# Seven block products instead of eight for half of the K chunks of gate, up and down in a decoder block

## The chip, the core and the metric

One core of a Trainium2 chip runs the whole kernel. The metric is the device time of one execution in microseconds. TensorE multiplies, VectorE (DVE) and ScalarE (ACT) do elementwise work, GpSimd (POOL) can do elementwise work on SBUF, and SyncE (SP) issues the loads.

## The reference

A decoder block for 256 tokens: two attention branches, gates, a merge, then a dense FFN and a last norm. The change concerns the FFN:

```python
hn = rmsnorm(h, ffn_norm[l])                                    # h (256, 2048)
h = h + (jax.nn.silu(hn @ w_gate[l]) * (hn @ w_up[l])) @ w_down[l]   # w_gate, w_up (2048, 5632), w_down (5632, 2048)
return rmsnorm(h, final_norm)
```

## The kernel before

All values are float32. Each product is made of three float32r passes: an operand is cut into hi (its float32r rounding) and lo = operand - hi, and hi*hi + lo*hi + hi*lo are summed in PSUM. The activations are the stationary operand, transposed, in tiles of 128 K rows by 128 tokens; there are two token tiles. The weights stream past them in slabs of 512 columns.

A *job* is one slab: its K rows (16 tiles of 128 in gate and up, 44 in down) for both token tiles, summed in two PSUM banks `acc`. A *step* is two K tiles of a job: 2 K tiles x 2 token tiles x 3 passes = 12 matmuls (L805 for hi of the weights, eight of them; L810 for lo, four). A *group* is four K tiles (two steps) loaded by one DMA of 1 MB into one of four `raw` buffers (`load`, L722). `split` (L731) makes the weights of one step ready: ScalarE casts `raw` to `wh` (L742) and VectorE subtracts to get `wl` (L743). There are four buffers each of `wh` and `wl`, and the split of step s + 3 is issued at step s, so it can start when step s - 1 is done with its buffer. The last split of a group frees `raw`, and the next load into it is issued.

The order on each engine is the order in which the Python loop at L789 issues: at each step first the split of step s + 3, then what `later(d, fn)` has put down for this step, then the matmuls. Each engine works through its own instructions in that order; an instruction that waits holds up all behind it on the same engine.

What comes after a slab: `wout_done` (L582) adds the output projection to h in `xt`, takes the sums of squares, and two and three steps later transposes h on TensorE (`transpose4`, tile `hT_tp`), from which ScalarE and VectorE make `hh` and `hl`. `gate_ff_done` puts silu of the gate slab into `sil`; `up_done` multiplies with the up slab, and two and three steps later `sil` is transposed (`aT_tp`) and cut into `ah`, `al`, which stay in SBUF for down. `down_done` adds to `xt`. The last six steps run for one token tile, then for the other (`TAIL`).

Of the kernel before, what the change touches and what calls it, by code (L numbers as in the profile page):

```python
# [62 lines left out]
def block_kernel(ctx: ExitStack, tc, x, positions, attn_norm, w_in, q_norm, w_uq, kv_norm, w_ukv,  # L63
# [8 lines left out]
    work = ctx.enter_context(tc.tile_pool(name="work", bufs=2))  # L72
# [14 lines left out]
    # ------------------------------------------------------------------ setup  # L87
# [25 lines left out]
    # mask: [tri | 0 | tri], added to scores [q, k]  # L113
    mask = const([P, 3, P], "mask")
# [17 lines left out]
    # ------------------------------------------------------------ small helpers  # L132
    def rstd(ss, n, name):
        """ss [P, NT, m] partial sums of squares over n elements -> [P, NT] of 1/rms, in two parts."""
# [20 lines left out]
    def split_out(src, hi, lo, scale=None):  # L155
        """src -> hi + lo (float32r), scale a [P, 1] factor per partition."""
# [7 lines left out]
    def transpose4(nat, hi, lo, name, key=None, k0=0, nk=4, j0=0, first=False):  # L164
        """columns j0*128 .. nk*128 of nat [P tok, NT, :] -> hi, lo [P, :, S] at the same j, times the gains."""
# [22 lines left out]

    def rope(o1, o2, x1, x2, c, s, shape, name):
# [72 lines left out]
    # ------------------------------------------------------------ streams  # L262
    jobs = []

    def job(w, kt, lhs, done, name):
        jobs.append(dict(w=w, kt=kt, n=w.shape[1], lhs=lhs, done=done, name=name))

# [10 lines left out]
    # ------------------------------------------------------------ phase 1: x -> xT, projections  # L278
# [22 lines left out]

    L = {}
# [63 lines left out]
    # ------------------------------------------------------------ attention  # L366
    yT = {}
    PT = [const([P, 2, 512], f"PT{i}", F32R) for i in range(2)]
# [66 lines left out]
    # MLA head pairs  # L435
# [76 lines left out]
    # MoBA: SEQ == MOBA_BLOCK, so every query's own block is block 0 and no past block exists  # L512
# [45 lines left out]
    # ------------------------------------------------------------ branches, merge, FFN  # L558
# [7 lines left out]
    mh, ml, hh, hl = [], [], [], []  # L566
    ssh = const([P, NT, 4], "ssh")
    ssf = const([P, NT, 4], "ssf")
    R["h"], h_root, h_invert = rstd(ssh, D, "rstd_h")

# [11 lines left out]
    def wout_done(c):  # L582
        def done(ps):
# [4 lines left out]
            hh.append(big([P, 4, S], f"hh{c}", F32R))  # L588
            hl.append(big([P, 4, S], f"hl{c}", F32R))
# [6 lines left out]
    ah, al_ = [], []  # L596

    def gate_ff_done(c):
        def done(ps):
            s = L["sil", c] = big([P, NT, 512], f"sil{c}")  # L600
            for t in range(NT):
                nc.scalar.activation(s[:, t], ps[t], AF.Silu, scale=R["h"][:, t:t + 1])
        return done

    def up_done(c):
        def done(ps):
            s = L["sil", c]
            for t in range(NT):
                nc.vector.scalar_tensor_tensor(s[:, t], ps[t], R["h"][:, t:t + 1], s[:, t], op0=OP.mult, op1=OP.mult)
            ah.append(big([P, 4, S], f"ah{c}", F32R))  # L610
            al_.append(big([P, 4, S], f"al{c}", F32R))
            spread(2, s, ah[c], al_[c], f"aT{c}")
        return done
# [10 lines left out]
    def down_done(c):  # L624
        def done(ps):
            h = xt[c]
            for t in range(NT):
                nc.vector.tensor_add(h[:, t], ps[t], h[:, t])
                sumsq(h[:, t], ssf[:, t, c:c + 1])
                nc.vector.tensor_mul(h[:, t], h[:, t], L["gf"][c // 2][:, c % 2])  # L630
        return done

    def begin_norm():
        nc.vector.tensor_reduce(out=vf, in_=ssf[:, :, 0:3], axis=mybir.AxisListType.X, op=OP.add)
        nc.vector.tensor_scalar(vf, vf, EPS * D, None, op0=OP.add)
        nc.scalar.activation(warm, warm, AF.Sqrt)

# [23 lines left out]
    # ------------------------------------------------------------ the list of products  # L661
# [32 lines left out]
    for c in range(11):  # L694
        job(w_gate[:, 512 * c:512 * (c + 1)], 16, lhs_of(hh, hl), gate_ff_done(c), f"ga{c}")
        job(w_up[:, 512 * c:512 * (c + 1)], 16, lhs_of(hh, hl), up_done(c), f"up{c}")
    for c in range(4):
        job(w_down[:, 512 * c:512 * (c + 1)], 44, lhs_of(ah, al_), down_done(c), f"dn{c}")

    # ------------------------------------------------------------ issue  # L700
    groups, steps = [], []
    for jb in jobs:
        jb["step0"] = len(steps)
        k0 = 0
        while k0 < jb["kt"]:
            nk = min(2 if len(groups) < 2 else 4, jb["kt"] - k0)
            gi = len(groups)
            groups.append((jb, k0, nk))
            for k in range(k0, k0 + nk, 2):
                steps.append(dict(job=jb, k0=k, g=gi, off=k - k0, end=k + 2 >= k0 + nk, toks=(0, 1), src=len(steps)))  # L710
# [3 lines left out]
    steps[-TAIL:] = [dict(st, toks=(t,)) for t in range(NT) for st in tail]  # L714
    step_of = {jb["name"]: jb["step0"] for jb in jobs}

# [3 lines left out]
    raws, splits = {}, {}  # L720
# [120 lines left out]
```

## Time and profile before

| what | us |
|---|---|
| three runs | 1343.98, 1344.4, 1344.5 (median 1344.4) |
| span of the profiled execution | 1342.6 |
| of it TensorE busy | 1327.8 |
| VectorE, ScalarE, GpSimd busy | 742.2, 629.8, 2.1 |
| gate and up | about 605 to 1093 |
| down | about 1094 to 1334 |

The median of the runs is 1.8 us above the profiled span. A row of the timeline gives the start, the busy time, the engine, the line of the kernel, the operation, the output and inputs by the program's names and their shapes; in square brackets stands the idle time in front of it and what ended that. A matmul's busy time overlaps the next one's, so starts, not durations, give the pace.

### The profile page before, as it was taken

The page shows a single profiled execution, that of the slowest core. Times are in us where ns is not written, and L with a number is a line of the kernel's source. Part 1 is how long each engine was busy: PE and PEld are TensorE (multiplying, and loading weights), DVE is VectorE, ACT ScalarE, POOL GpSimd, SP SyncE. Part 2 cuts the span into 40 slices and gives each one's busy share as a digit, 9 for nine tenths or more (in the row PEclk, how much of TensorE's full clock was granted, in tenths as well). Part 3 has the DMA queues.
Part 4 walks back from the last instruction along what each step waited for, and adds up shares of the span by engine and source line. Part 5 has one row for each costly group of instructions (what it writes and reads, how often), then busy time and mean ns, then how long its engine had stood idle before and what let it go on. Part 6 is the DMA issues. An engine that isn't in the chain of part 4 may idle for free.

```text
span 1342.6 us, 15600 instructions
## 1 busy us (share of the span) xinstructions
PE 1327.8 (99%) x6146; PEld 1107.6 (82%) x6146; DVE 742.2 (55%) x1017; ACT 629.8 (47%) x807; POOL 2.1 (0%) x11
## 2 busy tenths in 40 slices
PE   8999999999999999999999999999999999999997
PEld 6888888888888888888888888888888888888885
DVE  5766667574565566555554445444544454545453
ACT  6455555654444454546344444444444443434352
POOL 0000000000000000000000000000000000000000
PEclk9999999999999999999999999999999999999999
DMA  8565454455555555555565556656555565555551
GB/s 295 184 207 185 165 156 152 158 180 189 188 179 166 188 188 188 188 184 187 188 193 189 188 188 188 188 188 188 189 188 188 188 219 191 197 199 197 188 188 63
DMA packets 126966, 249.04 MB, mean 185 GB/s; under 512 B 4486, under 2 KB 9132, under 8 KB 126892
## 3 DMA queue, kind: packets, MB, share of 16 engines
q1 hardware_dynamic: 126620, 247.78, 56.7%
q8 instruction: 48, 0.79, 0.2%
q10 hardware_dynamic: 272, 0.26, 0.1%
q14 instruction: 26, 0.21, 0.1%
HBM read 245.93 MB, written 2.10 MB: 185 GB/s over the span
## 4 chain that ended last, share of the span: by engine, by line
PE 99%; DMA 0%; ACT 0%; DVE 0%; SPq 0%; ACTq 0%; issue 0%
PE acc L805 63%; PE acc L810 31%; PE aT_tp L170 1%; PE sb L382 1%; PE yb L418 0%; PE ya L418 0%; DMA x<-in_x_dram 0%; PE sa L382 0%; PE xT_tp L170 0%; PE mT_tp L170 0%; PE hT_tp L170 0%; PE pTa L405 0%; PE pTb L405 0%; PE kT_tp L170 0%; PE qn_tp L462 0%; PE qT_tp L170 0%
## 5 line engine op out<-in xcount | busy, mean ns | idle before, releaser
L743 DVE TENSOR_TENSOR wl<-raw,wh 128x1024 fp32r<-128x1024 f32 (+2 forms) x468 | 564.4, 1213 | 515.8 <-ACT wh L742 466.8
L742 ACT CAST wh<-raw 128x1024 fp32r<-128x1024 f32 (+2 forms) x468 | 486.2, 1043 | 547.5 <-PE acc L805 525.0
L805 PE MATMUL acc<-wh,hh 128*128 128x512 f32 x704 | 190.5, 392 | 0.0
L805 PE MATMUL acc<-wh,hl 128*128 128x512 f32 x704 | 188.4, 389 | 0.0
L810 PE MATMUL acc<-wl,hh 128*128 128x512 f32 x704 | 188.3, 389 | 0.0
L805 PEld LDWEIGHTS acc<-wh,hl 128*128 128x128 f32 x704 | 132.2, 188 | 27.9
L810 PEld LDWEIGHTS acc<-wl,hh 128*128 128x128 f32 x704 | 132.2, 188 | 27.6
L805 PEld LDWEIGHTS acc<-wh,hh 128*128 128x128 f32 x704 | 130.5, 188 | 25.9
L805 PE MATMUL acc<-wh,xh 128*128 128x512 f32 (+1 forms) x512 | 139.4, 394 | 0.0
L805 PE MATMUL acc<-wh,xl 128*128 128x512 f32 (+1 forms) x512 | 135.6, 387 | 0.0
L810 PE MATMUL acc<-wl,xh 128*128 128x512 f32 (+1 forms) x512 | 135.0, 386 | 0.0
L805 PEld LDWEIGHTS acc<-wh,xl 128*128 128x128 f32 x512 | 95.7, 189 | 19.8
L810 PEld LDWEIGHTS acc<-wl,xh 128*128 128x128 f32 x512 | 95.6, 189 | 19.4
L805 PEld LDWEIGHTS acc<-wh,xh 128*128 128x128 f32 x512 | 91.8, 189 | 15.2
L805 PE MATMUL acc<-wh,ah 128*128 128x512 f32 x352 | 95.3, 390 | 0.0
L805 PE MATMUL acc<-wh,al 128*128 128x512 f32 x352 | 95.1, 389 | 0.0
L810 PE MATMUL acc<-wl,ah 128*128 128x512 f32 x352 | 95.1, 389 | 0.0
L805 PEld LDWEIGHTS acc<-wh,al 128*128 128x128 f32 x352 | 66.1, 188 | 13.8
L810 PEld LDWEIGHTS acc<-wl,ah 128*128 128x128 f32 x352 | 66.1, 188 | 13.7
L805 PEld LDWEIGHTS acc<-wh,ah 128*128 128x128 f32 x352 | 65.9, 188 | 13.6
L153 ACT ACTIVATE junk<-x 128x512 bf16<-128x512 f32 (+1 forms) x26 | 15.5, 598 | 42.6 <-DVE x L643 18.1
L805 PE MATMUL acc<-wh,mh 128*128 128x512 f32 x128 | 35.1, 396 | 0.0
(262 smaller groups left out, 896.7 us busy)
## 6 DMA issues: line engine op xcount, KB each, us to landing
raw<-in_w_in_dram SPq DMA_DIRECT2D x59, 1024.0 KB, 5.1
raw<-in_w_gate_dram SPq DMA_DIRECT2D x44, 1024.0 KB, 5.2
raw<-in_w_up_dram SPq DMA_DIRECT2D x44, 1024.0 KB, 5.2
raw<-in_w_down_dram SPq DMA_DIRECT2D x44, 1024.0 KB, 5.1
raw<-in_w_out_dram SPq DMA_DIRECT2D x16, 1024.0 KB, 5.2
raw<-in_w_branch_b_dram SPq DMA_DIRECT2D x8, 1024.0 KB, 5.1
raw<-in_w_branch_a_dram SPq DMA_DIRECT2D x8, 1024.0 KB, 5.1
raw<-in_w_uq_dram SPq DMA_DIRECT2D x4, 768.0 KB, 4.6
```

The lines of the kernel that those rows point to most:

```text
L153: nc.scalar.activation(junk[:, :src.shape[-1]], src, AF.Square, accum_out=acc)
L170: nc.tensor.transpose(tp[:, k, t * P:(t + 1) * P], nat[:, t, (j + k) * P:(j + k + 1) * P], ident)
L382: nc.tensor.matmul(ps[:, t, :], lhsT=l, rhs=r, start=i == 0, stop=i == len(mm) - 1)
L742: nc.scalar.copy(hi, v)
L743: nc.vector.tensor_sub(lo, v, f32(hi))
L805: nc.tensor.matmul(accs[t], lhsT=jb["lhs"](k0 + k, t)[i], rhs=hi[:, k], start=i == 0 and k0 + k == 0, stop=False)
L810: nc.tensor.matmul(accs[t], lhsT=lh, rhs=lo[:, k], start=False, stop=last and k == 1)
```

## The change

Gate and up of the same columns become one job of two slabs (`pair`), and so do two neighbouring slabs of down. K is cut into chunks of four K tiles (512 rows). A chunk is taken as a 2 x 2 by 2 x 2 block product: the activations are a11, a12, a21, a22 (token tile by half chunk), the weights are half chunks of slab a and slab b. In an ordinary chunk ("N") this is eight block products of 6 matmuls each, in four steps of 12. In a seven-product chunk ("S") sums of blocks are multiplied: seven block products, named P1 to P7, in seven steps of 6 matmuls, each with weights of its own to be split. Four of the seven need weight sums T (four per chunk, made by GpSimd from `raw`, in four buffers), and three kinds of activation sums q (made by GpSimd from the uncut transposed activations, then cut by ScalarE and VectorE). P1, P5, P6 and P7 have PSUM banks of their own for a whole pair, and after the last S chunk `pair_sums` adds them into two SBUF tiles A and B, to which P2, P4, P3 and X are added at the end.

The order of the chunks is `GU_KINDS = "SSNN"` in gate/up (11 pairs) and `DN_KINDS = "SNSNSNSNSNN"` in down (2 pairs). The product of gate and up moves from VectorE to GpSimd. Down's activations are kept uncut (`aF`) and are cut anew for each of the two pairs of slabs by `feed`, eight steps ahead of the chunk. Before h is transposed, ScalarE scales its rows by an approximate 1/rms from the first 512 columns (`hr`), which `hs` corrects after the product. `TAIL` becomes 4. The attention part in front is as before.

The core of the diff:

```diff
+GU_KINDS = "SSNN"
+DN_KINDS = "SNSNSNSNSNN"
+    def turned(nat, F, name, j, key=None, k0=0, tag="tp"):
...
+                nc.tensor.transpose(tp[:, k, t * P:(t + 1) * P], nat[:, t, (j + k) * P:(j + k + 1) * P], ident)
+        if key is None:
+            nc.scalar.copy(F[:, j:j + 2, :], tp)
...
+    def cut(F, name, kind):
+        o = dict(n=[big([P, 4, S], name + x, F32R) for x in "hl"])
+        nc.scalar.copy(o["n"][0], F)
+        nc.vector.tensor_sub(o["n"][1], F, f32(o["n"][0]))
...
+        nc.gpsimd.tensor_add(q[:, 0], a21, a22)
+        nc.gpsimd.tensor_sub(q[:, 1], q[:, 0], a11)
+        nc.gpsimd.tensor_sub(q[:, 2], a11, a21)
+        nc.gpsimd.tensor_sub(q[:, 3], a12, q[:, 1])
+        def finish():
...
+            nc.scalar.copy(o["s"][0], q)
+            nc.vector.tensor_sub(o["s"][1], q, f32(o["s"][0]))
     def wout_done(c):
...
-            spread(2, h, hh[c], hl[c], f"hT{c}", "ffn", 4 * c)
+            d = 4 if c == 0 else 1
...
+                    nc.scalar.mul(st["n"][:, t], h[:, t], R["h0"][:, t:t + 1])
...
+            later(d, rows)
+            for i in range(2):
+                later(d + 1 + i, lambda i=i: turned(st["n"], st["F"], f"hT{c}", 2 * i, "ffn", 4 * c, "acc"))
+            later(d + 3, ready)
...
+    def gu_begin(c):
...
+            def gate():
+                A = st["A"]
+                for t, k in enumerate(("P2", "P4")):
+                    nc.vector.tensor_add(A[:, t], ps[k], A[:, t])
+                    nc.scalar.activation(A[:, t], A[:, t], AF.Silu, scale=hs[:, t:t + 1])
+                for t in range(NT):
+                    nc.scalar.mul(A[:, t], A[:, t], hs[:, t:t + 1])
+            def up():
+                B = st["B"]
+                for t, k in enumerate(("P3", "X")):
+                    nc.vector.tensor_add(B[:, t], ps[k], B[:, t])
+            def times():
+                nc.gpsimd.tensor_mul(st["A"], st["A"], st["B"])
...
+            later(ends["P4x"], gate)
+            later(ends["X"], up)
+            later(ends["X"] + 1, times)
+            for i in range(2):
+                later(ends["X"] + 5 + 3 * i, lambda i=i: turned(st["A"], aF[c], f"aT{c}", 2 * i, tag="acc"))
...
+        if kind == "S":
+            first = len(tsums)
+            tsums.extend((ga, gb, i) for i in range(4))
+            for key, g, off, a in (("P1", ga, 0, ("n", 0, 0)), ("P2", ga, 2, ("n", 1, 0)), ("P5", None, 0, ("s", 0, 0)),
+                                   ("P3", gb, 2, ("s", 3, 0)), ("P6", None, 1, ("s", 1, 0)),
+                                   ("P7", None, 2, ("s", 2, 0)), ("P4", None, 3, ("n", 1, 1))):
...
+    def make_sums():
+        while n_made[0] < min(len(tsums), n_cut[0] + SUMS):
...
+            nc.gpsimd.tensor_sub(T, x, y)
...
+    def feed(j, c):
+        def go():
+            aop[c], finish = cut(aF[c], f"d{j}_{c}", DN_KINDS[c])
+            if finish:
+                later(3, finish)
+        return go
+            at(f"dn{j}", u - 8, feed(j, c))
```

What stands where, at two places.

TensorE, where the activations of the first gate/up slab are transposed, before: one step into the next slab (`acc220`), behind VectorE's product `sil0`.

```order
L805 MATMUL acc220_0_5394<-wh220_5334,hl0_4592 128x512
L805 MATMUL acc220_1_5395<-wh220_5334,hl0_4592 128x512
L810 MATMUL acc220_0_5394<-wl220_5335,hh0_4591 128x512 [waits DVE_49]
...
L810 MATMUL acc220_1_5395<-wl220_5335,hh0_4591 128x512 x2
L170 MATMUL aT0_tp0_5412<-ident_87,sil0_5243 128x128 [waits DVE_49] x2
...
L805 MATMUL acc220_0_5394<-wh221_5350,hh0_4591 128x512 [waits Activation_49]
```

The same place now: five steps into the next pair, between P6 and P7 of its first chunk, behind GpSimd.

```order
L1029 MATMUL acc230_P6_5540<-wh230_5495,h0qh_4760 128x512 [waits Activation_49]
...
L1029 MATMUL acc230_P6_5540<-wh230_5495,h0ql_4761 128x512 x2
L1033 MATMUL acc230_P6_5540<-wl230_5496,h0qh_4760 128x512 [waits DVE_49]
...
L208 MATMUL aT0_tp0_5553<-ident_87,ga0_5334 128x128 [waits Pool_49]
...
L1029 MATMUL acc231_P7_5559<-wh231_5510,h0qh_4760 128x512 [waits Activation_49]
```

GpSimd at that place now (before it has no instruction there): `ga0` is the product of gate and up of the pair that has ended, T12 to T15 are the sums for the second chunk of the next pair.

```order
L925 TENSOR_TENSOR T12_5466<-raw116_5408,raw115_5371 128x1024 [waits DMAHW7_49,DMAHW6_49,DVE_49]
L925 TENSOR_TENSOR T13_5499<-raw116_5408,T12_5466 128x1024 [waits DVE_49,Pool_49]
L705 TENSOR_TENSOR ga0_5334<-ga0_5334,up0_5335 128x1024
L925 TENSOR_TENSOR T14_5514<-raw116_5408 128x1024 [waits DVE_49]
L925 TENSOR_TENSOR T15_5527<-raw115_5371,T13_5499 128x1024 [waits DVE_49,Pool_49]
```

The transposes have moved from one step of 12 matmuls to five steps of 6 behind the end of the slab, and from VectorE's product to one on GpSimd that has a weight sum ahead of it.

ScalarE in the first slab of down, before: casts of weights and, at a slab's end, sums of squares.

```order
L742 CAST wh403_8718<-raw204_8586 128x1024 [waits DVE_49,PE_49]
L742 CAST wh404_8736<-raw205_8620 128x1024 [waits DMAHW2_49,DVE_49,PE_49]
L153 ACTIVATE junk_103,ssf_129<-x0_79 128x512 [waits DVE_49]
L153 ACTIVATE junk_103,ssf_129<-x0_79 128x512 [waits DVE_49,Activation_49]
L742 CAST wh405_8758<-raw205_8620 128x1024 [waits PE_49]
```

ScalarE in the first pair of down now: `d0_4h` and `d0_4qh` are the cuts of the activations and of their sums q for chunk 4; `wh467` is the cast for the last step of chunk 3.

```order
L938 CAST wh463_9098<-T95_8918 128x1024 [waits DVE_49,PE_49]
L219 CAST d0_4h_9104<-aF4_6850 128x1024
L938 CAST wh464_9119<-raw199_8968 128x1024 [waits DMAHW4_49,DVE_49,PE_49]
L938 CAST wh465_9129<-raw200_8985 128x1024 [waits DMAHW5_49,DVE_49,PE_49]
L938 CAST wh466_9139<-raw199_8968 128x1024 [waits DVE_49,PE_49]
L232 CAST d0_4qh_9145<-d0_4q_9108 128x1024 [waits Pool_49]
L938 CAST wh467_9155<-raw200_8985 128x1024 [waits DVE_49,PE_49]
```

GpSimd's order for that q: the four sums for the weights of chunk 4 stand ahead of it.

```order
L925 TENSOR_TENSOR T96_9066<-raw202_9064,raw201_9026 128x1024 [waits DMAHW7_49,DMAHW6_49,DVE_49]
L925 TENSOR_TENSOR T97_9078<-raw202_9064,T96_9066 128x1024 [waits DVE_49,Pool_49]
L925 TENSOR_TENSOR T98_9090<-raw202_9064 128x1024 [waits DVE_49]
L925 TENSOR_TENSOR T99_9102<-raw201_9026,T97_9078 128x1024 [waits DVE_49,Pool_49]
L225 TENSOR_TENSOR d0_4q_9108<-aF4_6850 128x256 [waits PE_49]
L226 TENSOR_TENSOR d0_4q_9108<-d0_4q_9108,aF4_6850 128x256 [waits Pool_49]
```

Between the weight casts ScalarE now has casts that wait for GpSimd. The load of `raw202` waits for VectorE's cut of the previous S chunk's P3.

## Rows read from the trace of the kernel before

**Rows 1.** The page: span, TensorE's busy time, the chain that ended last.
```profile
span 1342.6 us, 15600 instructions
...
PE 1327.8 (99%) x6146; PEld 1107.6 (82%) x6146; DVE 742.2 (55%) x1017; ACT 629.8 (47%) x807; POOL 2.1 (0%) x11
...
PE 99%; DMA 0%; ACT 0%; DVE 0%; SPq 0%; ACTq 0%; issue 0%
```
**Rows 2.** Stretches: length, each engine's busy time (instructions), granted clock, DMA share, GB/s.
```profile
605.00:1093.00 488.00, 488.00 (x2196) 403.95 (x2195) 242.34 (x228) 215.31 (x229) 0.00 (x0) 1.00 0.59 189
1094.00:1330.00 236.00, 236.00 (x1047) 195.46 (x1046) 115.71 (x111) 96.59 (x107) 0.00 (x0) 1.00 0.53 179
```
**Rows 3.** Timeline in gate/up: start, busy us, engine, line, operation, tiles, count.
```profile
703.98 1.05 ACT L742 CAST wh<-raw 128x1024 fp32r<-128x1024 f32 x1 [1.67 <-PE acc L805]
...
704.69 1.07 PE L805 MATMUL acc<-wh,hh 128*128 128x512 f32 x4
705.07 1.23 DVE L743 TENSOR_TENSOR wl<-raw,wh 128x1024 fp32r<-128x1024 f32 x1 [1.50 <-ACT wh L742]
...
706.70 1.05 ACT L742 CAST wh<-raw 128x1024 fp32r<-128x1024 f32 x1 [1.67 <-PE acc L805]
```
**Rows 4.** Groups on TensorE: busy us, mean ns of one, idle.
```profile
L805 PE MATMUL acc<-wh,hh 128*128 128x512 f32 x704 | 190.5, 392 | 0.0
...
L805 PE MATMUL acc<-wh,ah 128*128 128x512 f32 x352 | 95.3, 390 | 0.0
```
**Rows 5.** Groups on VectorE and ScalarE, shapes apart, columns as in rows 4.
```profile
L743 DVE TENSOR_TENSOR wl<-raw,wh 128x1024 fp32r<-128x1024 f32 x452 | 550.2, 1224 | 501.3 <-ACT wh L742 456.7 <-PE acc L805 42.6 <-PE sb L382 1.5
...
L586 DVE TENSOR_TENSOR x<-acc,x 128x512 f32<-128x512 f32 x8 | 5.2, 686 | 3.4 <-PE acc L810 3.4
...
L742 ACT CAST wh<-raw 128x1024 fp32r<-128x1024 f32 x452 | 473.7, 1053 | 532.4 <-PE acc L805 509.8 <-issue 12.3 <-DMA raw<-in_w_in_dram 8.4
L602 ACT ACTIVATE sil<-acc,rstd_h 128x512 f32<-128x512 f32 x22 | 13.9, 686 | 22.0 <-PE acc L810 22.0
```
**Rows 6.** Timeline of GpSimd: its largest and last instructions, columns as in rows 3.
```profile
1.24 0.42 POOL L115 MEMSET mask<- 128x384 f32 x1
1.73 0.54 POOL L117 TENSOR_SCALAR_AFFINE_SELECT mask<-mask 128x128 f32<-128x128 f32 x2
2.21 0.56 POOL L370 MEMSET PT<- 128x256 f32 x2
```
**Rows 7.** Timeline behind a slab of the output projection.
```profile
580.89 1.29 DVE L586 TENSOR_TENSOR x<-acc,x 128x512 f32<-128x512 f32 x2 [0.86 <-PE acc L810]
581.14 1.07 PE L805 MATMUL acc<-wh,mh 128*128 128x512 f32 x4
...
582.91 0.19 ACT L153 ACTIVATION_READ_ACCUMULATOR junk<-x 128x1 f32 x1
...
583.00 1.98 ACT L742 CAST wh<-raw 128x1024 fp32r<-128x1024 f32 x2
583.87 0.60 PE L170 MATMUL hT_tp<-ident,x 128*128 128x128 f32 x4
```
**Rows 8.** DMA issues: count, KB each, median us from issue to landing.
```profile
raw<-in_w_up_dram SPq DMA_DIRECT2D x44, 1024.0 KB, 5.2
raw<-in_w_down_dram SPq DMA_DIRECT2D x44, 1024.0 KB, 5.1
```
**Rows 9.** Timeline of TensorE at the start of the program.
```profile
7.97 2.06 PE L805 MATMUL acc<-wh,xh 128*128 128x512 f32 x4
9.82 1.91 PE L805 MATMUL acc<-wh,xl 128*128 128x512 f32 x4
```

More of the change, by code (lines that the diff above doesn't have):

```diff
@@ L593, in done, with both @@
                 later(5, h_invert)
-        return done
[L596 to L613, printed above, removed]
+                def both():
+                    v = L["h0_v"]
+                    nc.vector.tensor_mul(hs, v, R["h0"])
+                    nc.vector.tensor_mul(hs, hs, R["h"])
@@ L715, in block_kernel @@
     step_of = {jb["name"]: jb["step0"] for jb in jobs}
+    for s, st in enumerate(steps):
+        jb = st["job"]
+        for key, _ in st["mm"]:
+            jb.setdefault("first", {}).setdefault(key, s)
+            jb.setdefault("last", {})[key] = s
+    for jb in jobs:
+        if "kinds" in jb:
+            l = {k: v - jb["step0"] + 1 for k, v in jb["last"].items()}
+            seven = jb["kinds"].rindex("S")
+            jb["ends"] = dict(X=l["X"], P4x=l["P4"],
+                              P4=sum(7 if k == "S" else 4 for k in jb["kinds"][:seven + 1]))
@@ L717, in at, with load @@
     def at(name, d, fn):
         later_q.setdefault(step_of[name] + d, []).append(fn)
-    raws, splits = {}, {}
-    def load(g):
+    raws, splits, uses, made = {}, {}, {}, {}
+    for s, st in enumerate(steps):
+        if st["src"] == s and st["g"] is not None:
+            uses[st["g"]] = uses.get(st["g"], 0) + 1
+    for ga, gb, i in tsums:
+        for g in ((ga, gb), (gb,), (gb,), (ga,))[i]:
+            uses[g] += 1
+    n_loaded, n_made, n_cut = [0], [0], [0]
+    def load():
+        g = n_loaded[0]
@@ L744, in split @@
         splits[s] = (hi, lo)
-        if st["end"]:
-            del raws[st["g"]]
-            load(st["g"] + RAWS)
-    load(0)
+        if g is None:
+            n_cut[0] += 1
+        else:
+            used(g)
+        make_sums()
+    load()
     load_x(256, 256, nc.sync)
-    load(1)
+    load()
     load_x(512, 512, nc.sync)
-    load(2)
+    load()
     load_x(1024, 512, nc.sync)
     load_x(1536, 512, nc.sync)
-    for g in range(3, RAWS):
-        load(g)
+    for _ in range(3, RAWS):
+        load()
     nc.sync.dma_start(posi, positions.rearrange("(t p) -> p t", p=P), allow_slow_non_contiguous=True)
@@ L784, in block_kernel, with close_attention @@
     at("cq", 9, x_invert)
+    def close_attention():
+        attn_ctx.close()
+        L["sums"] = ctx.enter_context(tc.tile_pool(name="sums", bufs=SUMS, reuse_waits="tile"))
+    at("wa0", 0, close_attention)
+    def feed(j, c):
[4 more added lines that the diff above has]
+        return go
+    u = 0
+    for c, kind in enumerate(DN_KINDS):
+        for j in range(2):
+            at(f"dn{j}", u - 8, feed(j, c))
+        u += 7 if kind == "S" else 4
@@ L795, in block_kernel @@
         if s < START:
             split_until(s + 2)
-        jb, k0, n = st["job"], st["k0"], st["job"]["n"]
-        if k0 == 0:
-            accs = [psum.tile([P, 512], F32, name=f"acc{s}_{t}", tag="acc")[:, :n] for t in range(NT)]
         hi, lo = splits[st["src"]]
-        last = k0 + 2 >= jb["kt"]
+        n = hi.shape[-1]
+        accs = jb["accs"]
+        for key, _ in st["mm"]:
+            if jb["first"][key] == s:
+                accs[key] = psum.tile([P, 512], F32, name=f"acc{s}_{key}",
+                                      tag="tp" if key in ("P1", "P5", "P6", "P7") else "acc")[:, :n]
@@ L802, in block_kernel @@
         for i in range(2):
             for k in range(2):
-                for t in st["toks"]:
-                    nc.tensor.matmul(accs[t], lhsT=jb["lhs"](k0 + k, t)[i], rhs=hi[:, k],
-                                     start=i == 0 and k0 + k == 0, stop=False)
-        for t in st["toks"]:
+                for key, lhs in st["mm"]:
+                    nc.tensor.matmul(accs[key], lhsT=lhs(k)[i], rhs=hi[:, k],
+                                     start=i == 0 and k == 0 and jb["first"][key] == s, stop=False)
@@ L808, in block_kernel @@
+        for key, lhs in st["mm"]:
             for k in range(2):
-                lh, _ = jb["lhs"](k0 + k, t)
-                nc.tensor.matmul(accs[t], lhsT=lh, rhs=lo[:, k], start=False, stop=last and k == 1)
-        if last and jb is jobs[-1]:
-            last_done(st["toks"][0], accs[st["toks"][0]])
-        elif last:
-            jb["done"](accs)
-    assert not later_q, sorted(later_q)
+                nc.tensor.matmul(accs[key], lhsT=lhs(k)[0], rhs=lo[:, k], start=False,
+                                 stop=jb["last"][key] == s and k == 1)
@@ L818 @@
+        if "kinds" not in jb:
+            if jb["last"][1] == s:
+                jb["done"](accs)
+        elif jb is jobs[-1]:
+            for key, _ in st["mm"]:
+                if jb["last"][key] == s and key in ("P2", "P3", "P4", "X"):
+                    t = key in ("P4", "X")
+                    (last_slab if key in ("P2", "P4") else last_done)(int(t), accs[key])
+    for s in sorted(later_q):
+        assert not later_q[s], s
 _INS = ["x", "positions", "attn_norm", "w_in", "q_norm", "w_uq", "kv_norm", "w_ukv", "w_branch_a", "w_branch_b",
```

194 lines of the change are left out of this document (152 added, 42 removed).

## The prediction

> **What bounds the kernel now.** I read the page first: TensorE is busy for 99% of the span, and the chain that ended last is 99% TensorE [rows 1]. So every matmul taken away shortens the run, as long as nothing else makes TensorE wait. Then the stages: gate and up (605 to 1093 us) and down (1094 to 1330) have TensorE busy in all of it, VectorE about half, ScalarE about 43%, GpSimd not at all [rows 2]. The steady stretch shows why [rows 3]: twelve matmuls take 2.72 us (703.98 and 706.70 are two starts of the ScalarE cast), so one takes 0.227. ScalarE cuts the weights of a coming step in 1.05 us, starting 0.7 us before a step begins (703.98 against 704.69), VectorE follows with 1.23 us, and both then idle for 1.5. That idle time is the cover that the change draws on.
>
> I count in steps: S is a step of a seven-product chunk (6 matmuls, 1.36 us; 7 steps, 9.52), N one of an ordinary chunk (12 matmuls, 2.72 us; 4 steps, 10.88), S.0 the first step. Per pair of slabs a chunk before cost 48 matmuls, now 42 or 48.
>
> **The gain.** Each seven-product chunk saves 6 matmuls; there are 22 in gate/up and 10 in down, so 192 x 0.227 = 43.5 us. The groups agree: 3 x 704 / 8 for half of the chunks is 132, and 3 x 352 / 8 for five of eleven is 60 [rows 4]. Transposes stay 228.
>
> **What the cuts cost.** A seven-product chunk needs seven cuts instead of four. VectorE's 7 x 1.22 = 8.6 and ScalarE's 7 x 1.05 = 7.4 us [rows 5] still fit into 9.52; I take nothing. The cover left is 0.14 us a step on VectorE, so whatever else enters such a chunk shows.
>
> **GpSimd: the price that the trace doesn't have.** 128 sums of 128x1024, 11 products gate x up and 40 small sums go to an idle engine, which is never seen to add two tensors here. Bounds from its rows [rows 6]: it writes 128x384 in 0.42 us, so 1024 columns take 1.1; it reads and writes 128x128 (the two selections, 0.54) in 0.27, so 1024 take 2.2. Below 1.1 nothing speaks for it. A sum reads and writes, like the second row, so I take p = 2.2 us per sum, and keep 1.1 for the range.
> The Trainium skill (GPSIMD Engine Reference, Performance versus the Vector engine) has a float32 add of 2048 elements at 4497 ns on GpSimd, twice VectorE's; halved, an estimate of 2.25 us, by which the result would come out 2 to 3 us higher. No run here shows it yet.
>
> **New waits, ahead of gate.** Before, hT's transposes waited for VectorE's add only. Now ScalarE scales the rows first, behind two sums of squares and a cast. At 581.14 a slab starts [rows 7]; ScalarE's squares end at 583.1, the cast at 584.1, and two scalings, 2 x 0.69 [rows 5], at 585.4; the transposes stand at 583.87, so TensorE waits 1.6 us. This holds for two slabs; the last one meets 1.36 us steps and waits 1.6 + 1.36 = 2.9. The first slab is delayed by four steps and hidden. Sum +6.1.
>
> **New waits, from pair to pair of gate/up.** aT's transposes stand behind P6, five S steps (6.8 us) into the next pair, and wait for GpSimd's product, which stands behind sum T13 (order above). Let t = 0 be S.0. The old pair's P2 and P4 end at -5.2; VectorE adds them after its cut by -2.5, ScalarE's two silus and two scalings (0.69 each) end at -0.4, and only then is S.2's cast done (0.6), so its VectorE cut ends at 2.0, S.3's at 3.1, the two adds of the up half at 4.4 (0.69 each), S.4's at 5.6. T13 takes T9's buffer, which S.4's cut reads last: T13 runs from 5.7 to 5.7 + p, the product to 5.7 + 2p = 10.1. With 0.1 for the signal TensorE waits 2p + 5.8 - 6.8 = 3.4 us, more than the 2.7 that the pair saves. Ten pairs: +34.
>
> **New waits in down.** T sums need the second raw slab, whose load starts when S.3's cut (two chunks earlier) ends, at 1.6, and lands 5.2 later [rows 8]: 6.9 with the signal.
> - First chunk of the first down pair: the eleventh product stands behind two such sums, so it ends at 6.9 + 3p = 13.5, TensorE waits 6.8.
> - The four small sums q of the next seven-product chunk stand behind four T sums: they end at 6.9 + 4p + 4p/4 = 17.9. ScalarE's copy of q was issued at S.6 and stands in line, in front of the cast for the last step of the ordinary chunk. That cast ends 2.1 us (two of 1.05) after q, at 20.0; the step is due at 9.52 + 8.16 = 17.7. TensorE waits 2.3. After such a wait the casts come back to back, the cut that frees the slab ends at 4.7 instead of 1.6, the load lands at 9.9, and the wait is 5.3. Four a pair of slabs, the first of the first pair hidden by the 6.8: 2.3 + 5.3 + 5.3, and 2.3 + 3 x 5.3, together 31.1.
> - The q of chunk 0, twice, in the two ordinary chunks ahead: load 7.2, end 18.2 + 2.1 = 20.3 against 19.0, +1.3 each. The leaving of the first pair, with GpSimd's adds to x ahead of it: about 2.
> Sum 6.8 + 31.1 + 2.6 + 2 = +42.5. The tail is as before.
>
> **Sum.** Span 1342.6 - 43.5 + 6.1 + 34 + 42.5 = 1381.7. The median lies 1.8 above the span (1344.4), so **1384 us**: the matmuls go, and TensorE waits for GpSimd instead.
>
> **Clock.** It is granted in full (2.4 GHz) everywhere in the two stages [rows 2]. Only at the start, after TensorE's idle time, does a group of four matmuls take 2.06 us instead of about 1.07 [rows 9], some 1.8 us lost over eight (whether by the clock the rows don't say: they note it as full there too). If each wait over 5 us brought that back, eight of them would add 14. I take nothing, since no row shows a wait in the midst of work; the 14 belongs to the range.
>
> **Rivals.**
> 1. *GpSimd is quick* (p = 1.1). Then the pair wait is 2 x 1.1 - 1.0 = 1.2 (10 times, 12), the first down chunk 6.9 + 3.3 + 0.1 - 6.8 = 3.5, q ends at 6.9 + 5.5 = 12.4 and needs no wait: 1342.6 - 43.5 + 6.1 + 12 + 3.5 + 1.8 = 1322 or, with every wait hidden, 1301. For it: the memset row, and that GpSimd has nothing else to do. Against it: a sum reads two streams. It wins below about p = 1.7, where down's waits vanish and the pairs' (2.4 each) cost less than the matmuls saved.
> 2. *VectorE and GpSimd take turns* when both read two tensors from SBUF. VectorE is 90% full with such cuts in a seven-product chunk. A pair wait would then hold about three cuts of 1.22 more (10 x 3.6 = 36), and each of some eight down waits as many (29): 1384 + 65 = 1449. For it: nothing in the trace, where GpSimd works only in the first 3 us [rows 6]; against it likewise. It is decided by the mean of the cut while a T sum runs, 1.22 or more.
> The Trainium skill states this rule (SBUF — State Buffer, Who interferes with whom): a VectorE instruction with two SBUF inputs and a GpSimd instruction that reads SBUF block each other whole.
> 3. *The waits are smaller than the order suggests*, since T13 or q start sooner than I have them: half of the pairs' and down's waits, 1342.6 - 43.5 + 6 + 38 + 1.8 = 1345, no change. This needs two chains to be wrong at once.
>
> **How the numbers follow.** A measurement here tells 0.2% (2.7 us) from no change. Forecast 0.41, rival 1 0.36 (its fully hidden end included), rival 2 0.18, rival 3 0.05. Faster 0.36 + 0.02 = 0.38; same 0.03; slower 0.59. The signs are both likely: the forecast's own range is 1360 to 1405 (p from 1.9 to 2.3, plus the clock). The whole one reaches from 1315, below rival 1, to 1435, which leaves out the hidden end and most of rival 2.
>
> **What the new profile would show.** T sums at 2.2 us and not 1.1; TensorE waiting on GpSimd in front of aT_tp, 3.4 us each, and ScalarE waiting on GpSimd in front of qh in down; TensorE's busy share near 93%; cuts still at 1.22 us (rival 2: clearly more, and down longest). I would be wrong if the product ends before TensorE's fifth step, or if q is done by the time that its copy is due.

## The result, and the profile after

The changed kernel takes 1523.95 us (median of four runs, 1523.11 to 1527.39) against 1344.45 for the kernel before on the same chip: a ratio of 1.134 with a 95% interval from 1.132 to 1.135. It is slower, as forecast, but by 180 us where 40 were forecast, and outside of the range (1315 to 1435).

The page of the changed kernel, to be laid beside [rows 1]: span, busy time of each engine, the granted clock in 40 slices.

```profile
span 1521.1 us, 16111 instructions
...
PE 1345.2 (88%) x5954; PEld 1101.3 (72%) x5954; DVE 1098.8 (72%) x1198; ACT 780.7 (51%) x985; POOL 485.5 (32%) x202
...
PEclk9999999999999999999999999999999798978889
```

The 192 matmuls are gone (5954 instead of 6146), and yet TensorE is busy for longer: 1345.2 against 1327.8 - 43.5 = 1284.3 by the pace of before, so 60.9 us more than the matmuls that are left took before; these are called slower matmuls below. The rest of the span is idle: 1521.1 - 1345.2 = 175.9, where the kernel before had 1342.6 - 1327.8 = 14.8, so 161.1 of new waits. Added up: 1342.6 - 43.5 + 161.1 + 60.9 = 1521.1. These two numbers, new idle time and slower matmuls, are used for every run below.

By stage, gate/up and down, columns as in [rows 2]:

```profile
607.60:1179.10 571.50, 486.71 (x2069) 392.97 (x2068) 481.90 (x342) 296.78 (x327) 314.42 (x102) 0.93 0.49 161
1179.10:1511.50 332.40, 259.54 (x1006) 204.66 (x1004) 225.54 (x180) 157.19 (x175) 148.89 (x77) 0.87 0.38 133
```

Gate/up takes 571 us instead of some 490, down 332 instead of 240. TensorE is idle for 84.8 us of the first and 72.9 of the second. The granted clock is no longer 1.00.

What TensorE waits for (total us, times, longest):

```profile
PE aT_tp L208 <- POOL ga L705: 70.6, 11, 11.9
PE acc_P L1029 <- ACT wh L938: 55.3, 11, 7.2
PE acc_P L1033 <- DVE wl L939: 24.3, 18, 4.0
PE hT_tp L208 <- ACT hr L650: 5.7, 6, 3.2
```

The places are those of the forecast (`aT_tp` behind GpSimd's product, late weights in down, `hT_tp` behind ScalarE), the third row is not.

The groups that tell why: sums T on GpSimd, cuts on VectorE (busy us, mean ns).

```profile
L925 POOL TENSOR_TENSOR T<-raw,T 128x1024 f32<-128x1024 f32 x64 | 200.1, 3127 | 20.7 <-DVE wl L939 19.0
...
L939 DVE TENSOR_TENSOR wl<-raw,wh 128x1024 fp32r<-128x1024 f32 x420 | 627.4, 1511 | 220.3 <-ACT wh L938 203.3 <-PE acc L1029 9.1 <-PE acc_X L1033 3.4
```

A sum takes 3.1 us in the mean instead of the 2.2 assumed, and a cut 1.51 instead of 1.22 [rows 5], though neither does more work. One stretch of the two timelines shows it, first GpSimd, then VectorE:

```profile
592.79 2.40 POOL L925 TENSOR_TENSOR T<-raw,raw 128x1024 f32<-128x1024 f32 x1 [20.62 <-DMA raw<-in_w_up_dram]
595.26 3.26 POOL L925 TENSOR_TENSOR T<-raw,T 128x1024 f32<-128x1024 f32 x1
598.49 3.38 POOL L925 TENSOR_TENSOR T<-raw 128x1024 f32<-128x1024 f32 x1
```
```profile
594.37 1.90 DVE L939 TENSOR_TENSOR wl<-raw,wh 128x1024 fp32r<-128x1024 f32 x1 [2.00 <-ACT wh L938]
596.19 3.42 DVE L220 TENSOR_TENSOR h2l<-hF,h2h 128x1024 fp32r<-128x1024 f32 x1
599.53 3.42 DVE L939 TENSOR_TENSOR wl<-raw,wh 128x1024 fp32r<-128x1024 f32 x1
```

Alone, a sum takes 2.40 (592.79 to 595.19). The first cut that meets it starts at 594.37 and ends 1.08 after the sum has ended. The second sum then ends about 2.3 after that cut, and so on: from there both take 3.4, about 2.3 + 1.1, as if one stood while the other worked, and one cut passes per sum. In the whole trace the 149 cuts of 128x1024 that overlap work of GpSimd take 2.43 us in the mean, the other 399 take 1.22. An addition that takes one of its two inputs from PSUM isn't held up (a pair of them at 811.43, in the midst of a sum):

```profile
810.39 3.38 POOL L925 TENSOR_TENSOR T<-raw,T 128x1024 f32<-128x1024 f32 x1
```
```profile
811.43 1.27 DVE L694 TENSOR_TENSOR ga<-acc_P,ga 128x512 f32<-128x512 f32 x2
```

### The profile page after: what moved, and what is told of

It is laid out like the page before. It is cut to its first block, busy times and chain, and to the rows that moved or that the text cites. A ratio compares the mean times of both kernels' runs of the same rounds, so it can differ in the third digit from the quotient of the medians.

```text
span 1521.1 us, 16111 instructions
## 1 busy us (share of the span) xinstructions
PE 1345.2 (88%) x5954; PEld 1101.3 (72%) x5954; DVE 1098.8 (72%) x1198; ACT 780.7 (51%) x985; POOL 485.5 (32%) x202
## 5 line engine op out<-in xcount | busy, mean ns | idle before, releaser
L939 DVE TENSOR_TENSOR wl<-raw,wh 128x1024 fp32r<-128x1024 f32 (+1 forms) x436 | 641.5, 1488 | 234.9 <-ACT wh L938 212.5
L938 ACT CAST wh<-raw 128x1024 fp32r<-128x1024 f32 (+1 forms) x436 | 450.0, 1040 | 322.5 <-PE acc L1029 160.4
L939 DVE TENSOR_TENSOR wl<-T,wh 128x1024 fp32r<-128x1024 f32 x128 | 210.8, 1677 | 42.0 <-ACT wh L938 39.3
L925 POOL TENSOR_TENSOR T<-raw,raw 128x1024 f32<-128x1024 f32 x32 | 98.1, 3064 | 405.8 <-DMA raw<-in_w_up_dram 198.7
L925 POOL TENSOR_TENSOR T<-raw,T 128x1024 f32<-128x1024 f32 x64 | 200.1, 3127 | 20.7 <-DVE wl L939 19.0
L938 ACT CAST wh<-T 128x1024 fp32r<-128x1024 f32 x128 | 131.9, 1049 | 42.4 <-PE acc_P L1029 35.6
L925 POOL TENSOR_TENSOR T<-raw 128x1024 f32<-128x1024 f32 x32 | 102.0, 3187 | 1.2 <-DVE rstd_h_v L151 1.2
L208 PE MATMUL aT_tp<-ident,ga 128*128 128x128 f32 x88 | 18.8, 353 | 70.6 <-POOL ga L705 70.6
L1029 PE MATMUL acc_P<-wh,h3h 128*128 128x512 f32 x132 | 41.3, 394 | 4.9 <-ACT wh L938 4.9
L1029 PE MATMUL acc_P<-wh,h3l 128*128 128x512 f32 x132 | 41.1, 393 | 0.0
L1029 PE MATMUL acc_P<-wh,h2h 128*128 128x512 f32 x132 | 40.6, 389 | 0.0
```

The source lines that it names most:

```text
L208: nc.tensor.transpose(tp[:, k, t * P:(t + 1) * P], nat[:, t, (j + k) * P:(j + k + 1) * P], ident)
L925: nc.gpsimd.tensor_sub(T, x, y)
L938: nc.scalar.copy(hi, v)
L939: nc.vector.tensor_sub(lo, v, f32(hi))
L1029: nc.tensor.matmul(accs[key], lhsT=lhs(k)[i], rhs=hi[:, k], start=i == 0 and k == 0 and jb["first"][key] == s, stop=False)
```

## The experiments

The theories at the start. *Length*: the loss comes from GpSimd's durations and from what stands behind them in order, as in the prediction's sum. *Turns*: it comes from VectorE and GpSimd blocking each other (rival 2).

**Stand-ins for the sums.** Three runs replace each sum T by work on GpSimd that hardly reads: a subtraction over 8 of 512 columns, and memsets. All three leave the sums T out; order, cuts and matmuls are the changed kernel's.

```diff
-            nc.gpsimd.tensor_sub(T, x, y)
+            nc.gpsimd.tensor_sub(T[:, :, 0:8], x[:, :, 0:8], y[:, :, 0:8])
+            nc.gpsimd.memset(T[:, :, 8:512], 0.0)      # e2: once, e1: twice
+            nc.gpsimd.memset(T[:, :, 8:256], 0.0)      # e8: once, and this
```

> Each weight sum T on GpSimd is replaced by a subtraction of 8 columns (it keeps the waits) and two writes of zeros over the rest, so that GpSimd is about as long at it (2 x 1.05 us by the 0.42 us of 384 columns) but hardly reads; the weight sums are left out of the computation. Taking turns (VectorE's cuts with two SBUF inputs and GpSimd's reads exclude each other): the cuts fall back from 1.5-1.7 to about 1.25 us and the time to what was forecast without that, 1365 to 1400 us. Rival (the order of the waits and GpSimd's length do it, whoever shares what): the length is nearly kept, so most of the loss stays, 1480 to 1520 us.

> As the run before, with one write of zeros instead of two: GpSimd needs about 1.1 us per weight sum and hardly reads; the weight sums are left out. Taking turns: 1315 to 1340 us (1322 was worked out for p = 1.1). Rival (GpSimd's length in the order of the waits): about half of the loss stays, 1420 to 1460 us.

> Each sum T is replaced by a subtraction over 8 of the 512 columns and two memsets of the rest and of half of it, so that T lasts about 0.75 + 1.05 + 0.55 = 2.35 us, as long as a sum that runs alone, but does not keep VectorE's cuts waiting (sums are left out). The order is that of the changed kernel. If only GpSimd's own duration counted, as the prediction had it, its sum at p = 2.35 would be 1384 + 10 x 2 x 0.15 + some 8 in down = 1395, and with the 9 us that pairs cost without any sum (the run with pairs only) 1404. Between the stand-ins of 1.8 us (1396) and 2.9 us (1451) lies 1423. The rest up to the changed kernel's 1524, 100 to 120 us, is then what taking turns costs. If taking turns costs nothing, this run stands at 1510 or more.

Measured, by the length of a T's work in the trace (from its first start to its last end, in the mean): T of 1.5 us: 1395.6; of 2.3: 1437.0 (1436.0 to 1438.6); of 2.6: 1450.8. (The third expectation calls the first and the last 1.8 and 2.9, which the traces don't bear out.) The first two expectations had given a range to each theory, and the times lie between the two, so neither theory alone is right; the third lies between its 1404 and its 1510. A lone sum takes 2.34 to 2.41, between the last two runs. The waits and the cuts of the run at 2.3:

```profile
PE aT_tp L208 <- POOL ga L705: 47.9, 11, 10.4
PE acc_P L1031 <- ACT wh L940: 34.1, 11, 5.7
...
PE acc_P L1035 <- DVE wl L941: 2.1, 4, 0.7
```
```profile
L941 DVE TENSOR_TENSOR wl<-raw,wh 128x1024 fp32r<-128x1024 f32 x420 | 533.6, 1283 | 253.4 <-ACT wh L940 235.9 <-PE acc L1031 9.1 <-PE sb L430 1.5
```

The cuts are back at 1.28 us, and 87 us of 1524 are gone though GpSimd's work has nearly the same length; with T longer than a lone sum it is still 73. So the turns of the sums T cost 73 to 87 us here. What the products and the small sums q add, which still read in these runs, was not measured. One thing else differs and was not separated: a stand-in is done with its slab after its short subtraction, and 20 loads of the changed kernel wait for a sum as the last reader of their buffer (44.9 us of the load queue's waiting), 10 of the run at 2.3 (16.9 us). Length matters too: from 1.5 to 2.6 us the time rises by 55.

**All sums on VectorE**, and **only the product on VectorE.**

```diff
-            nc.gpsimd.tensor_sub(T, x, y)          # and every other nc.gpsimd add, sub, mul
+            nc.vector.tensor_sub(T, x, y)
```
```diff
-                nc.gpsimd.tensor_mul(st["A"], st["A"], st["B"])
+                nc.vector.tensor_mul(st["A"], st["A"], st["B"])
```

> All sums, the product of gate and up and the adds to x go from GpSimd to VectorE, everything else as in the changed kernel. Taking turns: VectorE does in 1.2 us what cost 3.3 on both, so this is faster than with GpSimd's help: a gate/up pair needs 31 x 1.22 + 8 x 0.69 = 43.4 us of VectorE against 40.8 of TensorE, a pair of chunks in down 18 x 1.22 + 4 x 0.35 = 23.4 against 20.4, in all 1366 us (1355 to 1400). Rival (too much work, wherever it is done): the load is moved to the fuller engine, 1500 us or more.

> Only the product of gate and up goes back to VectorE; the sums stay on GpSimd. TensorE's waits ahead of aT_tp (70.6 us in the trace) should end. Taking turns: the cuts stay slow and part of it comes back as waits for wl and wh, 1455 to 1495 us. Rival (the order of the waits): all of it is gained, 1450 us or less.

Measured: 1514.6 and 1507.9. Both moved little. The first lies where its rival had it (1500 or more), the second above both of its ranges. Without GpSimd the cuts take 1.22 us, and VectorE stands in its own queue instead, before sums whose second slab has not landed:

```profile
DVE T L925 <- DMA raw<-in_w_up_dram: 79.3, 12, 7.8
DVE T L925 <- DMA raw<-in_w_down_dram: 56.8, 10, 7.8
```

Behind each such sum stand the cuts, so TensorE waits for `wl` (108.8 us). With only the product moved, `aT_tp` waits 4.4 instead of 70.6 us, and `wl` 62.9 instead of 24.3: most of the wait changed its name.

```profile
PE acc_P L1033 <- DVE wl L939: 62.9, 47, 4.0
PE aT_tp L208 <- DVE ga L705: 4.4, 11, 0.4
```

**The same work in a later order.** Product ahead of sum T13, both transposes at step 8, the copy of q three steps later.

```diff
-            later(ends["X"] + 1, times)
+            later(ends["X"], times)
...
-                later(ends["X"] + 5 + 3 * i, lambda i=i: turned(st["A"], aF[c], f"aT{c}", 2 * i, tag="acc"))
+                later(ends["X"] + 8, lambda i=i: turned(st["A"], aF[c], f"aT{c}", 2 * i, tag="acc"))
...
-                later(3, finish)
+                later(6, finish)
```

> All work of the changed kernel stays, GpSimd's sums included; only the order moves: the product of gate and up goes ahead of sum T13, its two transposes are issued eight steps into the next pair (before: five and eight), ScalarE's copy of q three steps later. If single late instructions are what costs (the 70.6 us in front of aT_tp, the 127 us in which ScalarE stands at qh and the 50 us of casts late behind it), the product is ready some 3 us before it is needed and half of the q waits go: 1524 - 64 - 45 - some 20 to 30 of slower matmuls behind them = 1385 to 1420. If VectorE and GpSimd taking turns is what costs, a pair of slabs of gate/up cannot get below 22 cuts x 1.22 + 9 x 2.4 = 48.4 us (measured in the changed kernel: 51.3) and two chunks of down not below 14 cuts x 1.22 + 4 x 2.4 + 4 x 0.72 = 29.6 (measured 29.2 to 33): 1475 to 1495.

Measured: 1504.3, above the ranges of both theories and nearer to that of taking turns. Of the eleven waits at `aT_tp` behind the product one is left, 6.9 us long. GpSimd in the later order, the start of two pairs in a row, then TensorE's waits:

```profile
698.75 2.41 POOL L925 TENSOR_TENSOR T<-raw,raw 128x1024 f32<-128x1024 f32 x1 [18.84 <-DMA raw<-in_w_up_dram]
...
749.60 2.41 POOL L925 TENSOR_TENSOR T<-raw,raw 128x1024 f32<-128x1024 f32 x1 [18.60 <-DMA raw<-in_w_up_dram]
```
```profile
PE acc_P L1033 <- DVE wl L939: 73.2, 45, 4.1
...
PE aT_tp L208 <- POOL ga L705: 6.9, 1, 6.9
```

A pair takes 50.9 us, as in the changed kernel (51.3), against 40.8 of TensorE work. Between two pairs GpSimd idles for 18.6; in the other 32 its nine large operations take 2.4 (the first) and 3.3 to 3.4 us (the others) with one gap of 3.2, and the cuts pass one by one. So in gate/up it isn't a late instruction that costs but the rate: while sums run, a cut takes 3.4 us and a step of TensorE 1.36. Turns, there.

**Pairs alone.** No seven-product chunk at all, all else of the change kept (the rest of the diff leaves out the sums and takes silu's input and the up half straight from PSUM; transposes use the other four PSUM banks).

```diff
-GU_KINDS = "SSNN"
-DN_KINDS = "SNSNSNSNSNN"
+GU_KINDS = "NNNN"
+DN_KINDS = "NNNNNNNNNNN"
```

> No chunk is taken with seven products: all 6 x 16 matmuls of before are there, without sums T and q. The rest of the change stays: pairs of slabs, the rows scaled on ScalarE before the transposes, the product on GpSimd, the activations of down cut anew for each pair. (The transposes use the other four PSUM banks.) If the loss lies in the seven-product chunks, only the 5.4 us of the output projection are left: 1348 to 1354. If pairs and the product on GpSimd cost by themselves (a wait at aT_tp without any sum in front of it), 1365 or more.

Measured: 1359.3 (ratio 1.011), between the two forecasts: 8.6 us of new idle time, 2.9 of it at `hT_tp`, and 5.8 of slower matmuls. The part not foreseen is the border of the two pairs of down, where TensorE needs the PSUM banks that VectorE empties (last two numbers: idle time and releaser):

```profile
1226.78 0.47 PE L1035 MATMUL acc_P<-wh,d_0h 128*128 128x512 f32 x1 [2.01 <-DVE x L744]
1228.83 0.80 PE L1035 MATMUL acc_X<-wh,d_0h 128*128 128x512 f32 x1 [1.58 <-DVE x L744]
```

The step from here to 1524, 165 us although 192 matmuls go, belongs to the seven-product chunks.

**Fewer of them.** One chunk of four (three of eleven in down): once with GpSimd in the later order (transposes at steps 7 and 8), once all on VectorE in the changed kernel's order.

```diff
-GU_KINDS = "SSNN"
-DN_KINDS = "SNSNSNSNSNN"
+GU_KINDS = "SNNN"
+DN_KINDS = "SNNNSNNNSNN"
```

> One chunk of four instead of two is taken with seven products (three of eleven in down), in the later order: 17 such chunks a run of pairs, 17 x 6 x 0.227 = 23 us less TensorE work than before. Taking turns costs only where VectorE and GpSimd together have no time: here 19 x 1.22 + 5 x 2.4 = 35.2 us of 42.2 in a pair, so by turns as a matter of capacity 1344 - 23 + 5 = 1326. If it is each seven-product chunk that costs, as in the changed kernel (223 us lost over 32 chunks, 7.0 each, perhaps half of it with the later order), 1344 - 23 + 17 x 3.5 to 7.0 = 1380 to 1440.

> The same one chunk of four, with all sums and the product on VectorE and the order of the changed kernel. VectorE has 19 x 1.22 + 5 x 1.2 + 10 x 0.69 = 36 us to do in a pair of 42.2. If only capacity counts, 1326. If it is sums T that wait for a load in the midst of VectorE's queue (as in the run with all sums on VectorE, which lost some 6.7 us on each seven-product chunk), 1344 - 23 + 17 x 6.7 = 1435.

Measured: 1411.5 and 1384.2. Both are far above 1326, so a count of an engine's work per pair doesn't tell the time. A reading that these runs don't test: sums and cuts meet within one chunk, and it is there that the three steps of weights cut ahead run out. VectorE alone does better than two engines by turns, though the two runs differ in their order too. Its waits for slabs are still there (61.1 + 35.0 us in 17 chunks), and the time lies between the two forecasts, 1326 and 1435.

**Sums where their data is.** As the last, but a sum is issued two cuts after the issue of the load of its second slab, and one behind each cut instead of four in a row.

```diff
+            if n_split[0] < max(due[ga], due[gb]) or not only[0]:
+                return
```

> One chunk of four with seven products (three of eleven in down), everything on VectorE as in the run at 1384; only the place of the sums T in VectorE's queue changes: two cuts after the load of their second slab was issued, and one sum behind each cut instead of four in a row. If sums that wait for a load were what cost (96 us of such waits on VectorE there), the run falls to that with pairs only less the matmuls saved: 1359 - 23 = 1336, up to 1345. If the pile of work at the border of two pairs is what costs (four adds from PSUM, the product and seven cuts together on VectorE), it stays at 1365 or more.

Measured: 1351.1 (1350.9 to 1352.0). VectorE's waits for slabs, now:

```profile
DVE T L933 <- DMA raw<-in_w_up_dram: 4.7, 6, 1.2
DVE T L933 <- DMA raw<-in_w_down_dram: 4.3, 4, 2.2
```

33 us came from the place of 68 instructions in one queue; the forecast for that was 1336 to 1345, so not all of it went as expected. It is near the kernel before (ratio 1.0051, 1.0036 to 1.0066) and not yet below it.

**The seven-product chunk second in its pair** ("NSNN"; the transposes of h and, but for the last pair, of the product use the other four PSUM banks).

> The same, and in gate/up the seven-product chunk is the second of a pair instead of the first, so that its seven cuts no longer meet the adds at the end of the pair before. If the border was a cost in the run before, this one is faster by it: 1336 if both costs are gone, 8 us less than the kernel before the change. If it is the sum of VectorE's work in the seven-product chunks that costs (7 x 1.22 = 8.6 in 9.52 us and nothing else may enter), it is like the run before.

Measured: 1407.6, a miss: neither 1336 nor 1351. An ordinary chunk in front needs all four `acc` banks in its first two steps, and these wait for the old pair's last additions:

```profile
PE acc_P L1040 <- DVE up L702: 40.2, 10, 4.4
```

So of these two orders the better one has the chunk first that needs two of these banks later, which is the seven-product one.

**Two waits of the border.** On the run at 1351: second transposes at step 7, before X's bank is due, and at the end of the first pair of down only the additions at once.

```diff
-                later(ends["X"] + 5 + 3 * i, lambda i=i: turned(st["A"], aF[c], f"aT{c}", 2 * i, tag="acc"))
+                later(ends["X"] + 5 + 2 * i, lambda i=i: turned(st["A"], aF[c], f"aT{c}", 2 * i, tag="acc"))
...
                     nc.vector.tensor_add(h[:, t], ps[k], h[:, t])
-                    sumsq(h[:, t], ssf[:, t, 2 * j + i:2 * j + i + 1])
-                    nc.vector.tensor_mul(h[:, t], h[:, t], L["gf"][j][:, i])
+                    later(8 + 2 * i + t, rest)          # rest: these two
```

> The run at 1351 (one chunk of four, all on VectorE, sums spread) with two of its remaining waits taken away. The second transposes of a pair are issued one step earlier (seven instead of eight into the next pair), so that X's PSUM bank, which they use first, is free when X begins: 44.4 - 43.8 = 0.4 seen and about 0.9 of refilling, eleven times, 10 to 15 us. At the border of the two pairs of down only the adds that free PSUM are done at once; squares and the gain of the last norm come eight steps later: 1.9 + 1.5 + 3.2 of waits and some 4 of slower matmuls behind them, up to 10. If these waits were on the path, 1327 to 1340, less than the 1344.5 of the kernel before; if others take their place, 1345 to 1351.

Measured: 1335.1 (1333.7 to 1335.9), ratio 0.9930 (0.9917 to 0.9944): 0.7% below the kernel before, and the only run below it. The two edits were not run apart. Its page and the stretch of gate/up:

```profile
span 1333.7 us, 15892 instructions
...
PE 1309.5 (98%) x6044; PEld 1089.4 (82%) x6044; DVE 960.2 (72%) x1259; ACT 735.7 (55%) x935; POOL 2.1 (0%) x11
```
```profile
607.00:1080.00 473.00, 470.68 (x2109) 388.92 (x2108) 363.76 (x363) 263.99 (x293) 0.00 (x0) 1.00 0.57 193
```

17 chunks save 102 matmuls, 23.1 us; 9.4 of new idle time (5.6 at `hT_tp`) and 4.8 of slower matmuls are left: 1342.6 - 23.1 + 9.4 + 4.8 = 1333.7.

All runs, the times as medians, the last two columns from the profiled execution:

| run | us | new idle | slower matmuls |
|---|---|---|---|
| changed kernel | 1524 | 161.1 | 60.9 |
| all sums on VectorE | 1515 | 150.4 | 64.8 |
| only the product on VectorE | 1508 | 144.8 | 63.0 |
| later order | 1504 | 142.8 | 58.0 |
| stand-ins of 2.6 us | 1451 | 99.3 | 46.5 |
| stand-ins of 2.3 us | 1437 | 92.9 | 42.2 |
| stand-ins of 1.5 us | 1396 | 63.0 | 30.8 |
| pairs alone | 1359 | 8.6 | 5.8 |
| quarter, later order | 1412 | 61.3 | 29.2 |
| quarter, all on VectorE | 1384 | 40.3 | 21.1 |
| quarter, spread | 1351 | 19.0 | 11.7 |
| quarter, spread, "NSNN" | 1408 | 54.9 | 33.1 |
| quarter, spread, border | 1335 | 9.4 | 4.8 |

## Why the prediction fell short, by its own steps

The sign, the bound and most places were right: TensorE bound before, matmuls saved, waits for GpSimd in their place; the waits for `wl` were not among them. The size wasn't. Of its signs, T at 2.2 us and cuts at 1.22 did not come, the wait at `aT_tp` is 5.9 us instead of 3.4, and TensorE's busy share is 88% instead of 93%. What it had named as proof of being wrong, a product or a q that is ready in time, did not come either: the waits are longer than forecast, not shorter. In the prediction's terms, against the span of 1381.7 that it had summed up:

- **The gain**, 43.5: the matmuls left are the number forecast. What wasn't forecast is that the others get slower.
- **hT's transposes**, 6.1: measured 5.7. Right.
- **GpSimd's duration**, p = 2.2: a lone sum takes 2.34 to 2.41, so the row of the selections was the right one of the two to take. The Trainium skill's figure (GPSIMD Engine Reference, Performance versus the Vector engine), 2.25 us as an estimate, lies 4 to 7% below these rows. The small sums q take 0.72, not p / 4 = 0.55: four of them, 0.7 us a chunk.
- **Pair to pair**, 2p + 5.8 - 6.8: the chain was right. With T at 2.3 us and no turns the run with stand-ins waits (47.9 - 10.4) / 10 = 3.75 where the formula gives 3.7 to 3.8. In the changed kernel it is (70.6 - 11.9) / 10 = 5.9, since T13, the product and the cuts between them hold each other up. One of these borders:

```profile
824.68 3.32 POOL L705 TENSOR_TENSOR ga<-ga,up 128x1024 f32<-128x1024 f32 x1
```
```profile
825.72 6.67 DVE L939 TENSOR_TENSOR wl<-raw,wh 128x1024 fp32r<-128x1024 f32 x2
```
```profile
828.05 1.11 PE L208 MATMUL aT_tp<-ident,ga 128*128 128x128 f32 x4 [5.88 <-POOL ga L705]
828.82 1.20 PE L1029 MATMUL acc_P<-wh,h0qh 128*128 128x512 f32 x2
829.82 1.05 PE L1029 MATMUL acc_P<-wh,h0ql 128*128 128x512 f32 x2
830.67 1.02 PE L1033 MATMUL acc_P<-wl,h0qh 128*128 128x512 f32 x2
831.52 0.63 PE L1029 MATMUL acc_P<-wh,h0h 128*128 128x512 f32 x2
```

- **Down**, 42.5: the circle was the one described. GpSimd starts when the slab lands, ScalarE stands at the copy of q until GpSimd is done, the cuts then come back to back, and only the late one frees the slab:

```profile
1399.25 3.48 POOL L925 TENSOR_TENSOR T<-raw,raw 128x1024 f32<-128x1024 f32 x1 [15.36 <-DMA raw<-in_w_down_dram]
...
1412.85 0.72 POOL L228 TENSOR_TENSOR d_4q<-aF,d_4q 128x256 f32<-128x256 f32 x1
1428.04 4.88 POOL L925 TENSOR_TENSOR T<-raw,raw 128x1024 f32<-128x1024 f32 x1 [14.46 <-DMA raw<-in_w_down_dram]
```
```profile
1413.61 1.04 ACT L232 CAST d_4qh<-d_4q 128x1024 fp32r<-128x1024 f32 x1 [13.71 <-POOL d_4q L228]
```
```profile
1414.68 1.23 DVE L233 TENSOR_TENSOR d_4ql<-d_4q,d_4qh 128x1024 fp32r<-128x1024 f32 x1 [10.87 <-ACT d_4qh L232]
```

From the landing to the end of q it is 14.3 us where 5p = 11.0 were put down, and the period 28.8 where 20.4 + 5.3 = 25.7 were: the difference is nearly all GpSimd's. Elsewhere in down the same eight operations, at 1330.31 to 1342.71 with VectorE idle, take 12.4.
- **Both stages without turns.** In the run with stand-ins of 2.3 us TensorE is idle for 41.8 us of gate/up and 47.8 of down, where the prediction put down 34 (and a part of hT's 6.1) and 42.5; in the changed kernel it is 84.8 and 72.9. So the sum of waits was near for engines that don't hold each other up.
- **VectorE's cover of 0.14 us a step**, taken as enough: this is the step that failed. It was read with GpSimd idle. A cut beside a sum takes 3.4 us, so four of a chunk's seven cuts alone, one beside each of its four sums, take longer than the chunk (13.6 against 9.52). Rival 2 had this mechanism, with a chance of 0.18 and a price of 65; its price, by the stand-ins, was 73 to 87 us, and that includes the matmuls slowed behind its waits. It was argued over waits only, about three cuts to each, not as a rate that holds while sums run. The Trainium skill's rule (SBUF — State Buffer, Who interferes with whom), that the two block each other whole, stood in the prediction, and the trace now agrees: 3.42 and 3.38 us for operations that take 1.22 and 2.40 alone. With no row for or against it, the rule should have had the larger chance.
- **The clock**, taken as nothing, with 14 in the range: this is the second step that failed, and the one that no rival had. The granted clock around the border above (stretch, length, TensorE busy, clock):

```profile
822.00:828.00 6.00, 0.17 (x1) 0.72 0.11 42
828.00:830.00 2.00, 1.95 (x7) 0.50 0.00 0
830.00:832.00 2.00, 2.00 (x8) 0.62 0.00 0
832.00:836.00 4.00, 4.00 (x21) 1.00 0.10 8
```

During a wait of 5.88 us it fell to one half (1.2 GHz), and it stayed there for the first matmuls behind it: from 828.05 to 831.52 TensorE did four transposes and six matmuls, at the full pace 0.36 + 6 x 0.227 = 1.72 us, so 1.75 were lost. Ten of the eleven waits at `aT_tp` look like this one. Over the whole execution the trace's record of the granted clock has it at one half during 97.7 us of TensorE's busy time, so the clock took about half of that, 48.9 of the 60.9 us of slower matmuls. The other 12 fall at the full clock and stay open, and no run takes the clock by itself. The prediction counted eight waits at 1.8, and then left them out because no row showed a wait in the midst of work. [Rows 9] showed a price of that size, though there the clock is noted as full.

The sum: forecast span 1381.7; waits 92.9 instead of 82.6 without turns, + 10.3; slower matmuls + 42.2, which is the stand-in run's 1434.2; turns + 68.2 of waits and + 18.7 of slower matmuls: 1521.1. The share given to turns rests on the stand-in of 2.3 us, which is a little shorter than a lone sum; by the one of 2.6 us it is 73 to 76 instead of 86.9.

## What to carry to other kernels

An idle engine isn't free work: before moving tensor-by-tensor sums from VectorE's neighbourhood to GpSimd, count both engines' two-input SBUF work as one queue, as a rate over the stretch in which they overlap, and put a price on the lower clock behind TensorE's longer waits (here 1.75 us behind one of 5.9). When an operand of a queued instruction comes from a load, place the instruction by the landing, since all behind it on its engine waits too. Fewer multiplications pay only if the cuts and sums that they need come in time. Here one chunk in four did, by 0.7%, with everything on VectorE and the sums placed by the landing. Two in four were not run with that placing, nor was GpSimd, so whether more than one can pay stays open.

## What the runs showed of the hardware

- VectorE operations with two SBUF inputs and GpSimd sums pass one at a time (1.22 and 2.40 us alone, up to 3.4 each together); VectorE additions with a PSUM input keep their 0.64 to 0.69 us beside a sum; in the runs in which GpSimd mostly writes zeros, the cuts of slabs take 1.28 to 1.29 us in the mean.
- GpSimd's time doesn't follow the size downward: 128x1024 takes 2.40 us, 128x256 0.72, and 128x16 in the stand-ins, some of them beside cuts, still 0.44 to 0.89 in the mean.
- TensorE's granted clock fell to one half within a wait of 5.9 us and was back in full about 3.5 us after work began again.
